# Attention scores of two heads at once on the two row halves of the TensorE array

## The chip, the cores and the metric

The kernel runs on one NeuronCore of one Trainium2 chip. A core has a matrix engine (TensorE, written PE in the profile, with its weight loads shown as PEld), three engines for elementwise work (VectorE or DVE, ScalarE or ACT, GpSimd or POOL), a queue that issues transfers (SyncE or SP), a working memory (SBUF) of 128 partitions, and an accumulation memory (PSUM) of eight banks, each 128 partitions by 512 float32 columns. The metric is the device time of one execution in microseconds, taken as the median of several runs.

## The reference, cut to what matters

The program is one layer of a hybrid decoder: a feed-forward block, then a mixer of two branches (a gated linear attention, GLA, and a stick-breaking attention), then a second feed-forward block, with root-mean-square norms around each. It handles 512 prompt tokens with 16 meta tokens in front of them, and 8 running sequences of 4 new tokens each with 256 cached positions. The change touches the stick-breaking attention of the prompt, which has 16 heads of 64 dimensions:

```python
z = jnp.einsum('bqhd,bkhd->bhqk', qblk, k).astype(jnp.float32) * scale + bias_f
mask = k_idx[None, :] < qi[:, None]
l = jnp.where(mask, jax.nn.log_sigmoid(-z), 0.0)
r = lax.cumsum(l, axis=3, reverse=True) - l
a = jnp.where(mask, jnp.exp(jax.nn.log_sigmoid(z) + r), 0.0)
return jnp.einsum('bhqk,bkhd->bqhd', a.astype(v.dtype), v)
```

So for each head the score of a query and an earlier key is a product over 64 dimensions; its sigmoid is multiplied by the product of (1 - sigmoid) over all keys between the two. All tensors are float32.

## The kernel before

Float32 products are made on TensorE from the type fp32r. A value x is split in two parts: a high part, which is x cast to fp32r, and a low part, which is x minus the high part. A product of x and y is then high by high, high by low and low by high; the fourth is left out. The cast that makes a high part runs on ScalarE (`S.copy`) or VectorE, and the subtraction that makes the low part on VectorE (the helper `tt`, line 172, which is why so many rows of the profile carry L172).

The attention works on pairs of heads: `class Pair` (line 1902), eight pairs. The 128 rows of a pair's query, key and value matrices are two heads of 64 rows, head e = 0 in partitions 0 to 63 and head e = 1 in 64 to 127 (`own_`, line 1885). Projections fill most of TensorE's time in this stage: `tile_steps` (lines 728, 729 and 731 of the profile; queries) takes 8 steps of six matmuls, and `seven_steps` (lines 1079 to 1081; values and keys of one pair together, with seven products of half matrices in place of eight) 14 steps of six matmuls. The work of the pair before, everything between its scores and its weighted values, is placed between these steps.

Order is written out by hand. All of TensorE, VectorE, ScalarE and GpSimd run inside `manual_schedule`: each engine executes in the order in which the program emits its instructions. At each step of the projections the program emits six matmuls, then what `later(n, f)` has due (counted in steps from the call), then the list `at[n]`, whose entries are kept in the order in which they were registered with `then`. The loop at line 2555 registers, for pair `pr`, its own pieces at n + d with n = BEGIN[pr+1], and the weight preparation of the pair's projections at BEGIN[pr] + TILE + d. Two entries for one step stand in the order of the loop: the pieces of pair `pr` first, the weight preparation of pair `pr+1` after them. Of that preparation (`weights_at`, line 1041) three places matter here. The cast of the block called "b2" (128x1024, ScalarE, line 1006) is emitted at n + 10 and its low part (VectorE) at n + 11; the matmuls that read b2 first are those of step n + 15. A block called "t4" (128x512) is cast at n + 13 and its low part made at n + 15. The samples of the queries are copied at n + 11 (line 1926), and a partial sum of the projection, e5, at n + 12 on ScalarE (line 1059).

For the scores, each query block i of 128 tokens meets 144, 272, 400 or 528 keys (16 meta tokens and the tokens up to its own end), 1344 columns in all for a head, laid out in three PSUM banks of 416, 416 and 512 columns (`PARTS`, `BANKS`, lines 1868 to 1871). `scores(e, n)` (line 1996) makes bank n of head e: five segments of a head (144, 272, 400, 16 and 512 columns) with two matmuls each, 20 matmuls a pair. Each uses all 128 rows of the array. The query tile of a head holds its high part in the head's own 64 partitions and its low part in the other 64; the key tile holds the key's high part twice. One matmul therefore sums high by high and low by high. The second takes a tile `klz` with the key's low part in the head's own half and zeros in the other. So one pass of 64-row products is saved by stacking, at the price of copies between halves: `hi` and `lo` of the queries and `key_parts` of the keys each run twice, once a head, on 64 partitions.

Behind the scores come two sigmoids a bank on ScalarE (`keep` and `beta`, lines 2012 and 2013, `keep` with single columns zeroed by GpSimd), a running product along the keys on VectorE (`scan`, line 2026, in two parts of 416 and 928 columns), `weigh` (beta times the shifted product, 1343 columns, L172, then two copies of the meta columns, line 2036), and then ten 128x128 transposes a head (`turned`, line 2087) and the product with the values (`summed`, line 2103, at the third step of the next pair, followed by `meta_summed`, line 2118). `rows_v`, `rows_k` and `tails` (lines 2053, 2042, 2062 to 2064) transpose keys and values into output rows; `tails` is followed by four short VectorE operations (lines 2068 to 2075). The steps are:

```python
pieces = [(3, now.scores, 0, 0), (3, now.scores, 0, 1), (4, now.meta), (5, now.scan, 0, 0),
          (6, now.scores, 0, 2), (6, now.scores, 1, 0), (6, now.rows_v), (8, now.scan, 0, 1), (9, now.scan, 1, 0),
          (10, now.weigh, 0), (11, now.scores, 1, 1), (11, now.scores, 1, 2), (11, now.rows_k), (11, now.tails),
          (14, now.scan, 1, 1), (15, now.weigh, 1)]
```

`turned` follows at step 16 (first head) and 19 (second). For pairs 4 to 7 sixteen transposes of cached keys (`sample_keys`, line 2190) stand at step 14, and for pair 1 a few small matmuls (`sample_rows_out`, lines 2169 and 2171). So TensorE visits the scores three times a pair, at steps 3, 6 and 11. PSUM tiles of the kind `ps` rotate through four banks, and `scores` takes one at a time, two a visit.

Of the kernel before, what the change touches and what calls it, by code (L numbers as in the profile page):

```python
# [9 lines left out]
F32 = mybir.dt.float32  # L10
F32R = mybir.dt.float32r
# [5 lines left out]
P = 128  # L17
# [36 lines left out]
06481820500232254e646b6c0c808e2c42907a388c927e8884706846862a2e1478587644826e5436403e3c246a661e623a948a5b7c100e60545a  # L54
0072741416126a555628262034245a3202305e86462e5c50824458563c403676542a786e07491e3a948a0e62106674607c1812167a726c0c3892
2c708c42078488021d48406a1c238e687e04903c801e065207140900841f16506a231a4a513e681d483d527e19068e810a50214c8014120b183c
1c481e061f2350531968213e8e805117143c0a061281161822526a1e191b80403e1c8f06508e18810a162212401b206a1e3e23068e1a190a8050
1812211b0b6a1e400a0680231a208e181b126a13211420231e06088e0a8030606e7462568c34381a32428a7012667c2a92445a54244e78820f20
0d6c7e8a68483c167052183e0f4e206a500d4012584f0c50703f3d4041513e4f0c503c3d4f7141703c3d3e403f185a2a3e7012504d4a59665806
0a244e480f2894746042863c4456326e14928e6202000482487a5070160c124d7e7c0e1080390b33756187078c72466c0840263d36433f453c57  # L60
29909525676f6a2276784b308a3888544a68344d7e50369052374e843a202212706a4b384a4d367c7d226a4c366c0e804a10168c722e0c2a7c1a
7a1c5e92181e3c8e5c225a602c5707403e6e947466264228468c0a245956877208440c86756a2e1a0620629238406e18024a243e161e47808c1d
669474367210335e0a3a4c3259560e046c26751c7c7a071a946220802e000c385a8645666a8c10061e6044728e2c923c369333320e5c0b088274
5e06601e942220475f2a62581c287a6c7c09241a6a488c102b262c44928e7256576e168136804218747a64146b0b0402084c0e3e40327c866c28
3c8209101a5a8e728c669281566a26242b4236010c181000083b3e824c440e4a484d242826423c402c2e36010c48284618080a2b2411823e4d2e
0244043b42002c183c40080a36480c4200020411483b26824d180a2c2e2b4c39370824283e3c0c422b0037404336243b824a053c0a0818024539
3e11280e0c004c480440422b370c2826242f3e11484a36822d002b0c0e0a083c241802054244262b824c2d10360042251840043b3c2f484a102b
82000208260a24282d0e0c0536102b394c82403642002b0d183c3e3b3802000c39288236080e100a404a4c242639363e2882040c3c2b42364818
263e243c4345264202000c28408210484c0a080e824a26280c4004362b2d0a48943e1e284c42100c2f62185a925d1a2d803a3862944524080a43
3c585f2c4a06805c940e822648422a1e1862432c3e4062485a1a2e80925c45245d18431e4a2a425e5c2c620608621824940a82260e5e5a1a4562  # L70
5c182c48240e4c0c4a1e2810185c2a5e421a4582264428182e2c461e1f2010224846441c4c0c4a605e1e2a2e2c0e1928100c222f20261c188248
4c2a4a4644422e0e2c181c1f00281e8094830a1a063c109204083e373a0082405826281e203b38390236102200920c0e83382c6263245a820302
26629237002c823a05040212243060725e5c5a62644e847e687a8e76887c706e526c78030174666a8c8a9406420a2a864408804b912d8a181a3c
2c54561c3e49020048904636502a2c2d0e8220729222024486803903014b605810707c0c00946a0942028c400b08074b0174526e66008c786d6c
00067a7b8f8889768448730f93117d412e5a7e71610d21644c5c1e624e482a7e6c8a4a043c1a5602543e361878008c50908643121680846a9426
7628246e74442a66325282228e3058209240085a607a700d5d2f2e3b06125c347c3616733a140888116670432c723b190c2a151a060e0f125a2e
425c3618898838467313082c17431c44120e0a1b72193a5a7336881a435d0c5e5c061c2d2c18151214360a1b171a423a730e5c88897215181406
0c1d2d1c1a380b0e42372c8872163606145d895c1a1c0b060c0a37882c0e365d5c1b421072880608820a50928e6e867e6c48146204361a0c946a
248c303c0276204e2a5474582c2e42465a9056141236181e1a54161c0c44757454587490751912911d181c5490741d581c197559185a0c243875
40563e74373c1c5718594336509082945492  # L80
# [56 lines left out]
def hybrid_step(  # L137
# [1747 lines left out]
    own_, other = (slice(0, 64), slice(64, P)), (slice(64, P), slice(0, 64))  # L1885
# [16 lines left out]
    class Pair:  # L1902
# [9 lines left out]
        def queries(self):  # L1912
# [15 lines left out]
            def hi(e):  # L1928
                if e == 0:
                    self.qs = [take(NP, F32R) for _ in range(2)]  # L1930
                S.copy(self.qs[e][own_[e]], qf[own_[e], :NP])

            def lo(e):
                tt(self.qs[e][other[e]], qf[own_[e], :NP], self.qs[e][own_[e]].bitcast(F32), ALU.subtract)
                if e:
                    give(qf)

            for n, f in ((3, samples), (6, lambda: hi(0)), (8, lambda: lo(0)), (9, lambda: hi(1)), (11, lambda: lo(1))):
                later(n, f)

        def keys(self):
# [7 lines left out]
            for e in range(2):  # L1949
                self.key_parts(e)  # L1950
            self.sample_parts()

        def key_parts(self, e):
            kf = self.kf
            if e == 0:
                self.ks = [take(nk, F32R) for _ in range(2)]
                self.kl = klz
# [842 lines left out]
```

## Time and profile before

| what | value |
|---|---|
| median of 3 runs | 1483.24 us (1483.19 to 1483.31) |
| the profiled execution: its time, its span | 1483.86 us, 1482.2 us |
| granted TensorE clock | 0.999 |
| busy: PE, DVE, ACT, POOL | 1473.1, 1094.1, 819.7, 59.9 us |
| attention of the prompt, 585 to 812 us of the span: PE, DVE, ACT busy | 227.0, 189.7, 175.1 us |

Spans and starts are microseconds from the first instruction. A matmul's row gives its start, its length from start to the last result, and its tile's shape as rows*columns of the weights and partitions x columns of what streams through. Matmuls overlap: a 280-column matmul shows 0.29 us, but the next starts about 0.13 us after it. The cost of a piece of work in the stream is therefore read from the end of the matmul before it to the end of the first one behind it.

### The profile page before, as it was taken

To read this page: it belongs to the slowest core of one execution; us is meant where nothing else is said; L and a number is where in the kernel's file an instruction comes from. 1 tells how busy PE (TensorE), PEld (TensorE's weight loads), DVE (VectorE), ACT (ScalarE), POOL (GpSimd) and SP (SyncE) were. 2 spreads that over 40 slices of the span, in tenths; PEclk is the share of its full clock that TensorE was granted. 3 is DMA by queue.
4 is the path that set the end of the run, shared out by engine and by line. 5 is a ranking of instruction groups with operands and counts; after the bars stand their busy time and mean duration, and the time that the engine had idled before them with its cause. 6 is when DMAs were issued, how large, how long until landed. Compare 5 with 4: busy or idle time off the path is not lost.

```text
span 1482.2 us, 29733 instructions
## 1 busy us (share of the span) xinstructions
PE 1473.1 (99%) x11825; PEld 1427.4 (96%) x11825; DVE 1094.1 (74%) x1812; ACT 819.7 (55%) x1537; POOL 59.9 (4%) x177
## 2 busy tenths in 40 slices
PE   9999999999999999999999999999999999999998
PEld 8999999999999889999998999999999999999998
DVE  5888888855677866988887754776577898888544
ACT  7455545534565557777776544644564555455334
POOL 2000000000000111300100000000000000000000
PEclk9999999999999999999999999999999999999999
DMA  8133333324765687567677767334631333333253
GB/s 253 45 100 89 100 99 102 89 79 125 180 134 132 174 146 174 122 119 147 146 136 177 244 136 205 102 91 129 189 105 49 102 96 108 95 108 88 81 148 120
DMA packets 288540, 187.60 MB, mean 127 GB/s; under 512 B 10988, under 2 KB 266674, under 8 KB 288402
## 3 DMA queue, kind: packets, MB, share of 16 engines
q1 hardware_dynamic: 280706, 181.97, 46.1%
q0 software_dynamic: 7680, 3.74, 2.4%
q8 instruction: 93, 1.52, 0.4%
q14 instruction: 45, 0.37, 0.1%
q10 hardware_dynamic: 16, 0.00, 0.0%
HBM read 160.63 MB, written 25.03 MB: 125 GB/s over the span
## 4 chain that ended last, share of the span: by engine, by line
PE 95%; DVE 2%; ACT 2%; DMA 1%; issue 0%; DVEq 0%; SPq 0%; ACTq 0%
PE acc L1302 8%; PE acc L1300 8%; PE acc L1301 8%; PE acc L741 6%; PE acc L742 6%; PE acc L744 6%; PE acc L728 5%; PE acc L729 5%; PE acc L731 5%; PE acc L1079 4%; PE acc L1081 4%; PE acc L1080 4%; PE acc L1242 2%; PE acc L1239 2%; PE acc L1240 2%; PE ps L2103 1%
## 5 line engine op out<-in xcount | busy, mean ns | idle before, releaser
L172 DVE TENSOR_TENSOR room<-room,room 128x544 fp32r<-128x544 f32 (+13 forms) x473 | 303.6, 661 | 87.5 <-ACT room L808 18.7
L172 DVE TENSOR_TENSOR lo<-raw,hi 128x1024 fp32r<-128x1024 f32 (+1 forms) x207 | 248.0, 1199 | 74.1 <-ACT hi L1006 37.1
L1302 PE MATMUL acc<-room,lo 128*128 128x280 f32 (+1 forms) x896 | 259.7, 290 | 0.0
L1300 PE MATMUL acc<-room,hi 128*128 128x280 f32 (+1 forms) x896 | 259.5, 290 | 0.0
L1301 PE MATMUL acc<-room,hi 128*128 128x280 f32 (+1 forms) x896 | 259.2, 289 | 0.0
L1006 ACT CAST hi<-raw 128x1024 fp32r<-128x1024 f32 x114 | 119.5, 1052 | 142.1 <-PE acc L1301 49.2
L728 PE MATMUL acc<-room,hi 128*128 128x280 f32 x608 | 173.2, 302 | 0.2 <-DVE room L175 0.2
L1300 PEld LDWEIGHTS acc<-room,hi 128*128 128x128 f32 x896 | 168.6, 188 | 0.0
L1301 PEld LDWEIGHTS acc<-room,hi 128*128 128x128 f32 x896 | 168.6, 188 | 0.0
L1302 PEld LDWEIGHTS acc<-room,lo 128*128 128x128 f32 x896 | 168.5, 188 | 0.0
L729 PE MATMUL acc<-room,hi 128*128 128x280 f32 x608 | 163.5, 288 | 0.0
L1079 PE MATMUL acc<-room,hi 128*128 128x280 f32 x476 | 141.7, 298 | 1.1 <-ACT acc L1069 0.9
L172 DVE TENSOR_TENSOR lo<-room,hi 128x1024 fp32r<-128x1024 f32 x106 | 101.2, 955 | 52.4 <-ACT hi L1006 52.2
L1081 PE MATMUL acc<-room,lo 128*128 128x280 f32 (+1 forms) x476 | 138.3, 290 | 0.0
L1080 PE MATMUL acc<-room,hi 128*128 128x280 f32 (+1 forms) x476 | 138.1, 290 | 0.0
L706 ACT CAST hi<-raw 128x1024 fp32r<-128x1024 f32 (+1 forms) x93 | 93.6, 1007 | 75.6 <-issue 21.5
L1006 ACT CAST hi<-room 128x1024 fp32r<-128x1024 f32 x106 | 89.1, 840 | 82.1 <-PE acc L1301 61.0
L731 PE MATMUL acc<-room,lo 128*128 128x280 f32 x608 | 125.9, 288 | 0.0
L728 PEld LDWEIGHTS acc<-room,hi 128*128 128x128 f32 x608 | 114.4, 188 | 5.2 <-issue 3.8
L729 PEld LDWEIGHTS acc<-room,hi 128*128 128x128 f32 x608 | 114.6, 189 | 0.3
L741 PE MATMUL acc<-room,hi 128*128 128x280 f32 (+2 forms) x388 | 110.7, 295 | 0.0
L742 PE MATMUL acc<-room,hi 128*128 128x280 f32 (+2 forms) x388 | 108.9, 290 | 0.0
(413 smaller groups left out, 3554.2 us busy)
## 6 DMA issues: line engine op xcount, KB each, us to landing
raw<-in_w_in_dram SPq DMA_DIRECT2D x68, 256.0 KB, 5.5
raw<-in_ffn_w_gate_dram SPq DMA_DIRECT2D x64, 256.0 KB, 3.1
raw<-in_ffn_w_up_dram SPq DMA_DIRECT2D x64, 256.0 KB, 3.3
raw<-in_ffn_w_down_dram SPq DMA_DIRECT2D x36, 448.0 KB, 3.8
raw<-in_w_in_dram SPq DMA_DIRECT2D x29, 512.0 KB, 7.2
out_dram<-room SPq DMA_DIRECT2D x36, 256.0 KB, 4.2
room<-in_cache_k_dram SPq DMA_DIRECT2D x32, 256.0 KB, 7.1
room<-in_cache_v_dram SPq DMA_DIRECT2D x32, 256.0 KB, 5.2
```

Of the source, the lines that this page charges most:

```text
L172: (eng or V).tensor_tensor(out=out, in0=a, in1=b, op=op)
L728: T.matmul(acc[h][:, :w], hi[k], act.get(k, h, w)[0], start=(k == order[0]), stop=False, skip_group_check=True)
L729: T.matmul(acc[h][:, : wid[h]], hi[k], a[h][1], start=False, stop=False, skip_group_check=True)
L731: T.matmul(acc[h][:, : wid[h]], lo[k], a[h][0], start=False, stop=(k == order[-1]), skip_group_check=True)
L741: T.matmul(acc[h][:nw, : wid[h]], wh, a[h][0], start=(k == 0), stop=False)
L742: T.matmul(acc[h][:nw, : wid[h]], wh, a[h][1], start=False, stop=False)
L1006: S.copy(hi[:, :kt], src)
L1079: T.matmul(x[:, :n], hi, act_[k][0][:, :n], start=(first and k == 0), stop=False, skip_group_check=True)
L1081: T.matmul(x[:, :w], lo, act_[k][0][:, :w], start=False, stop=(k == 3), skip_group_check=True)
L1300: T.matmul(x[:, :QW], hi, act[k][0], start=(first and k == 0), stop=False, skip_group_check=True)
L1301: T.matmul(x[:, :QW], hi, act[k][1], start=False, stop=False, skip_group_check=True)
L1302: T.matmul(x[:, :QW], lo, act[k][0], start=False, stop=(k == 3), skip_group_check=True)
```

## The change

The scores use the array as two halves of 64 rows. The tiles of queries and keys keep both heads in their own partitions, one tile for the high parts and one for the low parts. For each segment three products are made (high by high, high by low, low by high), each as two matmuls of 64 rows, head 0 in rows 0 to 63 and head 1 in rows 64 to 127, into two different PSUM banks: 30 matmuls a pair in place of 20. The high and low parts are made with one instruction for both heads, 128 partitions at once, the copies between halves and the zeroed tiles `klz` fall away, and the cast of the keys moves from two on VectorE and two on ScalarE to one on VectorE. A visit to the scores now makes one bank for both heads, at steps 3, 6 and 10; `scan` is in three parts of 416, 400 and 528 columns, `weigh` in two, of 815 and 528 columns. `rows_k` and `tails` move from step 11 to 10. The byte string `PLACES`, which says where in SBUF each tile lies, is replaced as a whole and is left out here.

```diff
-    klz = [take(nk, F32R) for _ in range(2)]
-    for t in klz:
-        G.memset(t.bitcast(F32), 0.0)
...
+    own_ = slice(0, 64), slice(64, P)
+    AT, SCANS = (0, 416, 832), (slice(0, 416), slice(416, 816), slice(816, NW_))
...
-            def hi(e):
-                if e == 0:
-                    self.qs = [take(NP, F32R) for _ in range(2)]
-                S.copy(self.qs[e][own_[e]], qf[own_[e], :NP])
-
-            def lo(e):
-                tt(self.qs[e][other[e]], qf[own_[e], :NP], self.qs[e][own_[e]].bitcast(F32), ALU.subtract)
...
+            def hi():
+                self.qs = [take(NP, F32R) for _ in range(2)]
+                S.copy(self.qs[0], qf[:, :NP])
+
+            def lo():
+                tt(self.qs[1], qf[:, :NP], self.qs[0].bitcast(F32), ALU.subtract)
+                give(qf)
+
+            for n, f in ((3, samples), (6, hi), (9, lo)):
                 later(n, f)
...
-            src, ks = kf[own_[e], NS:], self.ks
-            V.tensor_copy(ks[e][own_[e]], src)
-            S.copy(ks[e][other[e]], src)
-            tt(klz[e][own_[e]], src, ks[e][own_[e]].bitcast(F32), ALU.subtract)
+        def key_parts(self):
+            src = self.kf[:, NS:]
+            hi, lo = self.ks = [take(nk, F32R) for _ in range(2)]
+            V.tensor_copy(hi, src)
+            tt(lo, src, hi.bitcast(F32), ALU.subtract)
...
-            for n, f in ((13, lambda: self.key_parts(0)), (15, lambda: self.key_parts(1)), (16, self.sample_parts)):
+            for n, f in ((14, self.key_parts), (16, self.sample_parts)):
...
-                T.matmul(o, qs[e][:, qc], ks[e][:, kc], start=True, stop=False)
-                T.matmul(o, qs[e][:, qc], kl[e][:, kc], start=False, stop=True)
+                for x, y in ((qh, kh), (qh, kl), (ql, kh)):
+                    for e, r in enumerate(own_):
+                        T.matmul(p[e][:, c : c + k1 - k0], x[r, qc], y[r, kc], start=(x is qh and y is kh), stop=(x is ql))
...
-        def weigh(self, e):
+        def weigh(self, e, n):
             beta, keep = self.wide[e]
-            tt(beta[:, : NW_ - 1], beta[:, : NW_ - 1], keep[:, 1:], ALU.mult)
+            a, b = ((0, 815), (815, NW_ - 1))[n]
+            tt(beta[:, a:b], beta[:, a:b], keep[:, a + 1 : b + 1], ALU.mult)
...
-            pieces = [(3, now.scores, 0, 0), (3, now.scores, 0, 1), (4, now.meta), (5, now.scan, 0, 0),
-                      (6, now.scores, 0, 2), (6, now.scores, 1, 0), (6, now.rows_v), (8, now.scan, 0, 1), (9, now.scan, 1, 0),
-                      (10, now.weigh, 0), (11, now.scores, 1, 1), (11, now.scores, 1, 2), (11, now.rows_k), (11, now.tails),
-                      (14, now.scan, 1, 1), (15, now.weigh, 1)]
+            pieces = [(3, now.scores, 0), (4, now.meta), (5, now.scan, 0, 0), (6, now.scan, 1, 0), (6, now.scores, 1), (6, now.rows_v),
+                      (8, now.scan, 0, 1), (9, now.weigh, 0, 0), (10, now.scan, 1, 1), (11, now.weigh, 1, 0),
+                      (10, now.scores, 2), (10, now.rows_k), (10, now.tails),
+                      (13, now.scan, 0, 2), (14, now.weigh, 0, 1), (15, now.scan, 1, 2), (16, now.weigh, 1, 1)]
```

More of the change, by code (lines that the diff above doesn't have):

```diff
@@ L78 @@
[L78 to L80 removed]
+365a540c320824203012147a62827c44426e6672026092886a708e6884947618801c7404864c2a5052904e1f2e066c8a48404a183e3c7e8c2a18
+10156446007828291a2e2a0c201e2c26322428682294840886041c744e527690181a8a803c4a487e386c368c3a5e5c5a643e55167846627c0002
@@ L2586, in hybrid_step @@
         then(n + 21, lambda: give(*qz[:2]))
-        then(n + 23, lambda: give(*vfm, *klz, once.pop("begun"), *(once.pop(t) for t in ("az", "am", "vm"))))
+        then(n + 23, lambda: give(*vfm, once.pop("begun"), *(once.pop(t) for t in ("az", "am", "vm"))))
         for n in range(1 - 2 * MIX0, 1):
```

108 lines of the change are left out of this document (49 added, 59 removed).

## The prediction

> **What bounds the kernel now.** I read the page first, then the busy times of the stretch in which the changed code runs, then the timelines of its engines. The page's busy times, and the windows (PE, PEld, DVE, ACT, POOL busy us, then clock, DMA share, GB/s):
>
> ```profile
> PE 1473.1 (99%) x11825; PEld 1427.4 (96%) x11825; DVE 1094.1 (74%) x1812; ACT 819.7 (55%) x1537; POOL 59.9 (4%) x177
> 585.00:812.00 227.00, 227.00 (x1849) 210.27 (x1849) 189.69 (x309) 175.10 (x338) 28.35 (x89) 1.00 0.67 141
> ```
>
> TensorE is busy for all of the 227 us, so time is won or lost in two ways only: by what its own stream costs, and by a wait put into it. ScalarE and VectorE lose three instructions a pair each (a query part and, of the keys, two copies here, a cast and a low part there), and VectorE gets four shorter ones more (two scans, two products). I cost both at nothing, since TensorE's stream covers them. Since the stage moves at PE's pace, order matters here more than load.
>
> **The three visits as they are**, pair 3 (timeline of PE: start, length):
>
> ```profile
> 665.41 0.41 PE L731 MATMUL acc<-room,lo 128*128 128x280 f32 x2
> 665.75 2.37 PE L2103 MATMUL ps<-room,room 128*64 128x512 f32 x16
> 668.06 0.50 PE L2118 MATMUL ps<-room,room 96*128 96x512 f32 x1
> ...
> 669.37 0.38 PE L728 MATMUL acc<-room,hi 128*128 128x280 f32 x1
> ...
> 671.46 0.41 PE L731 MATMUL acc<-room,lo 128*128 128x280 f32 x2
> 671.71 0.40 PE L2008 MATMUL ps<-room 128*128 128x512 f32 x1
> 671.95 0.40 PE L2009 MATMUL ps<-room,room 128*128 128x512 f32 x1
> 672.18 0.23 PE L2008 MATMUL ps<-room,room 128*128 128x144 f32 x1
> 672.66 0.60 PE L2053 MATMUL ps<-ident,room 128*128 128x128 f32 x4
> ...
> 676.78 0.29 PE L1081 MATMUL acc<-room,lo 128*128 128x280 f32 x1
> 676.91 0.34 PE L2008 MATMUL ps<-room,room 128*128 128x400 f32 x1
> 677.10 0.35 PE L2009 MATMUL ps<-room,room 128*128 128x400 f32 x1
> 677.28 0.17 PE L2008 MATMUL ps<-room,room 128*128 128x16 f32 x1
> 677.31 0.26 PE L2009 MATMUL ps<-room,room 128*128 128x16 f32 x1
> 677.42 0.48 PE L2008 MATMUL ps<-room,room 128*128 128x512 f32 x1
> 677.97 0.60 PE L2042 MATMUL ps<-ident,room 128*128 128x128 f32 x4
> ```
>
> From end to end: first 668.56 to 669.75, less 0.13 for the 280-column matmul behind it, 1.06 us; second 671.87 to 673.26, less 0.44 for four transposes of 0.11, 0.95; third 677.07 to 678.57, less 0.44, 1.06. Together 3.07 us a pair. The steps are 0.23 for 512 columns (671.71, 671.95, 672.18), 0.18 for 400 (676.91, 677.10, 677.28), 0.13 for 280 (676.78 to 676.91), which I take for 272 too, and never under 0.11 behind a short matmul (677.31 to 677.42), where the next weights are what is waited for; 144 columns get 0.11.
>
> **What a visit will cost.** The trace has no pair of 64-row halves. Its nearest rows are two 64-column halves side by side (L2103), and a matmul on a part of the rows (16 of them, L456); L804 and L805 give the price of plain float32:
>
> ```profile
> 611.54 0.64 PE L2103 MATMUL ps<-room 128*64 128x512 f32 x1
> 611.55 0.64 PE L2103 MATMUL ps<-room,room 128*64 128x512 f32 x1
> ...
> 385.20 0.29 PE L744 MATMUL acc<-room,lo 128*128 128x280 f32 x1
> 385.33 0.63 PE L804 MATMUL ps<-room,ones 128*128 128x280 f32 x2
> 385.80 0.64 PE L805 MATMUL ps<-room,ones 128*128 128x280 f32 x2
> 386.06 0.50 PE L741 MATMUL acc<-room,hi 128*128 128x280 f32 x1
> ...
> 484.08 0.41 PE L731 MATMUL acc<-room,lo 128*128 128x280 f32 x2
> 484.42 0.69 PE L456 MATMUL ps<-room 16*128 16x256 f32 x2
> 485.05 0.40 PE L728 MATMUL acc<-room,hi 128*128 128x280 f32 x1
> ```
>
> L804 and L805: 385.49 to 386.56, less 0.13, is 0.94 us for 4 x 280 columns, 0.84 ns a column. The column halves start 0.01 us apart, and the sixteen of a pair of heads (512, 384, 256 and 128 columns, twice each a head) take 665.82 to 668.56, less 0.23 for L2118, 2.51 us. One head's 2560 columns at 0.84 ns are 2.15, so the second head costs nothing; 0.36 is over. I take the same for row halves (bounds: one price for two heads, as here, and both heads in turn). L456: 484.49 to 485.45, less 0.13, is 0.83 us for 2 x 256 columns, which at 0.84 ns are 0.43. The other 0.40 us is what it costs to leave the whole array and come back: the stream runs dry and weights are loaded in the open, twice. No such cost shows between shapes of the whole array above. Bounds: nothing, and 0.40 a visit; I take 0.40, as L456 is the row with part of the rows.
>
> The Trainium skill, TensorEngine Tiling (Array Packing), section Key Properties, says that changing the tiling mode drains TensorE; the 0.40 us agrees, and it names no mode that is exempt.
>
> Sum of a pair, three products for each segment: first visit 3 x 0.11 + 3 x 0.13 = 0.72, second 3 x 0.18 + 2 x 0.11 + 0.01 = 0.77, third 3 x 0.23 = 0.69, and 3 x 0.40: 3.38 us against 3.07. So the visits lose 0.31 us a pair, **2.5 us** in eight. The three saved passes of 1344 columns are real; three drains a pair eat them.
>
> **What the new order costs.** The scores of the third bank now stand at step 10, in front of the cast of b2 on ScalarE, which is registered for step 10 by the next turn of the loop; before, the sigmoids came at 11, behind it. ScalarE, VectorE, PE, same pair:
>
> ```profile
> 672.38 0.69 ACT L2012 ACTIVATE room<-ps,sbb 128x512 f32<-128x512 f32 x1 [0.21 <-PE ps L2009]
> 676.68 1.06 ACT L1006 CAST hi<-raw 128x1024 fp32r<-128x1024 f32 x1
> 678.62 0.70 ACT L2012 ACTIVATE room<-ps,sbb 128x512 f32<-128x512 f32 x1
> 679.19 0.71 ACT L2013 ACTIVATE room<-ps,sbb 128x512 f32<-128x512 f32 x1
> 679.76 0.61 ACT L2044 COPY room<-ps 128x512 f32<-128x512 f32 x1
> ...
> 679.97 1.23 DVE L172 TENSOR_TENSOR lo<-raw,hi 128x1024 fp32r<-128x1024 f32 x1
> ...
> 681.32 0.33 PE L1081 MATMUL acc<-room,lo 128*128 128x280 f32 x1
> ```
>
> The b2 low part ends at 681.20 and its first reader (step 15, third matmul) starts at 681.32: 0.12 us to spare already. Let E be the moment at which the matmul behind the third visit starts (677.97 here). PE reached that reader 3.35 us after E, with three steps between; with one step more (six matmuls of 0.13) it is E + 4.13. ScalarE starts on the bank 0.20 after E (672.18, 672.38); four sigmoids of 0.57 (678.62, 679.19, 679.76), the copy of `rows_k` 0.47 (0.61 less the 0.14 by which such neighbours overlap), the cast 1.06, and VectorE's low part 1.23 give E + 5.24. PE waits **1.1 us**. Behind that cast on ScalarE stands the copy of e5, which the first matmul of step 15 waits for with 280 columns; VectorE's low part of 1.23 us, which runs beside it, takes longer, so it lies inside the same wait. VectorE then has the scan of 528 columns and the product of 528, which end in front of the fourth transpose of `turned` at step 16:
>
> ```profile
> L2026 DVE TENSOR_TENSOR_SCAN room<-room,room 128x928 f32<-128x928 f32 x16 | 33.3, 2084 | 0.0
> L2026 DVE TENSOR_TENSOR_SCAN room<-room,room 128x416 f32<-128x416 f32 x16 | 16.2, 1012 | 10.9 <-POOL room L2016 10.8
> L172 DVE TENSOR_TENSOR room<-raw,raw 128x512 f32<-128x512 f32 x9 | 6.2, 686 | 0.5 <-PE ps L2103 0.5
> 707.53 1.91 PE L2190 MATMUL ps<-ident,room 128*128 128x128 f32 x16
> 627.02 1.03 PE L2171 MATMUL ps<-ones,room 1*128 1x1 f32 x8
> ```
>
> The scan is 1.25 (1.01 plus 112 columns at 2.1 ns), the product 0.70, less 0.1 of overlap: E + 7.1, while PE, off again at 5.24, is there after four matmuls, a step and three transposes (0.52 + 0.78 + 0.33) at 6.9. Another 0.2; **1.3 us a pair** in all. Pairs 4 to 7 have L2190's 1.9 us at step 14, ahead of the reader: no wait there. Pair 1 has L2171 and its transpose, 1.1 us: 0.3 is left. So pairs 0, 2 and 3 pay 1.3 and pair 1 0.3, **4.2 us**. Bounds: nothing, and 1.3 in all seven pairs that have a b2 behind them, 9.1.
>
> The rest I cost at nothing. The six instructions that fall away on ScalarE and VectorE would give, without PE's cover, at most 6 x 0.69 us a pair (the 512-column row). Both heads' first scores now need all of the keys at step 3 and the cast comes one step later for head 0, but `summed` (2.4 us) stands ahead of them on PE. PSUM still gives two banks a visit, in the same turn. The new byte string of places moves no instruction.
>
> Sum: 2.5 + 4.2 = 6.7 us. The profiled execution had a span of 1482.2 us and a time of 1483.86, 1.7 around the span and 0.6 above the median of 1483.24; I expect 1488.9 of span, about 1490.6 for its time, and a median of **1490.0 us**.
>
> **Rivals.**
> R1, no wait at step 15: the order is as read, but ScalarE and VectorE have run further ahead than I give them. For it: PE waits nowhere in this stretch now. Against: the chain starts at scores that PE itself makes. 1483.2 + 2.5 = 1485.7.
> R2, the other side, changing to row halves is free. Place: both ends of each visit. Price: 24 x 0.40 = 9.6 us less, 1480.4, and some exposed loads back, 1481. It decides from 0.12 us a visit down, where 24 x 0.12 pays for what is left of the waits (6.7 - 9.6 + 24s = 0). For it: L456 is a matmul alone, without a partner. Against: L2103's 0.36, with partners.
> R3, the halves' weight loads are not hidden. Streams alone are 0.56 us for five segments (1344 columns at 0.42 ns), three times 1.68, plus 15 loads of 0.11, 1.65, plus 1.2: 4.53, 1.15 more a pair, 9.2 in eight: 1499.2. The row
>
> ```profile
> 677.10 0.19 PEld L2008 LDWEIGHTS ps<-room,room 128*128 128x128 f32 x1
> ```
>
> speaks against it: on the whole array a load starts while L2008's matmul of 676.91 (0.34 long) runs. The Trainium skill, TensorE: Matmul & The Clock Gate, section The mechanism, has loads overlap with running matmuls only where the row group differs; that is R3 for a half's second load; for the whole array the trace disagrees, and no run here shows it for halves.
> R4, the change doesn't do what it says: the heads run in turn. Then streams and steps double, 2 x 2.18 + 1.2 = 5.56, 2.18 more a pair: 1507.
> R5, R1 and R2 together: 1481 - 4.2 = 1477.
>
> **How the numbers follow.** Forecast 0.42, R1 0.16, R2 0.13, R3 0.12, R4 0.07, R5 0.06, 0.04 for what I don't see. A measurement here tells 0.2%, 3.0 us, from no change. Faster (below 1480.3): R5, a third of R2, some of the rest, 0.14. The same (to 1486.2): most of R1 and of R2, 0.21. Slower: 0.65. The range of 8 in 10 takes in R1, R2 and R3, 1481 to 1500; the forecast's own, with waits of 2 to 9 us, is 1487 to 1495.
>
> **What would show it.** Rows of 64*128 matmuls with both heads' starts 0.01 to 0.02 us apart (R4: a step of 0.11 or more); a visit of 1.1 to 1.2 us end to end with a dry PEld at both ends (R2: 0.7); PE waiting for VectorE's low part at L1081 once a pair in pairs 0, 2 and 3, near 1 us, and not in 4 to 7 (R1: none). I am wrong if the visits come out shorter than 1 us, or if PE waits at another place.

## The result and the profile after

The changed kernel takes 1492.2 us (median of 4 runs, 1492.2 to 1493.64) against 1483.23 us before (4 runs, 1483.19 to 1483.31): the ratio is 1.0063, 95% interval 1.0045 to 1.0080. It is slower, as forecast, by 2.2 us more than forecast (1490.0). The span of the profiled execution went from 1482.2 to 1490.5 us, 8.3 more; its time, 1492.2, is the median itself, while the profiled execution of before lay 0.6 above its median.

From the page of the changed kernel its busy line, and from the windows the same stretch as before (us, then PE, PEld, DVE, ACT, POOL busy, clock, DMA share, GB/s):

```profile
PE 1477.0 (99%) x11905; PEld 1421.8 (95%) x11905; DVE 1085.3 (73%) x1820; ACT 804.9 (54%) x1513; POOL 57.0 (4%) x175
585.00:812.00 227.00, 223.13 (x1807) 198.43 (x1806) 176.81 (x310) 156.24 (x302) 24.09 (x83) 1.00 0.65 132
```

The work that was to go is gone: VectorE is busy 8.8 us less, ScalarE 14.8 us less. None of it shows in the time: TensorE, which was busy for all of the 227 us, now stands idle for 3.9 of them. The view of TensorE's waits from 580 to 820 us (before: none) says for whom (total us, times, longest):

```profile
PE ps L2078 <- ACT room L2183: 1.7, 1, 1.7
PE acc L1081 <- DVE lo L172: 1.3, 3, 0.4
PE acc L1079 <- ACT room L1059: 0.7, 3, 0.3
```

The second was forecast, three times, in pairs 0, 2 and 3; the third stands in the same pairs, where the prediction had it inside the second. The first, once, in pair 7, was not forecast.

**Where the 8.3 us are.** The first matmul of `summed` (512 columns on column halves) ends the work of one pair and begins that of the next, so its start is a milestone. Timelines of TensorE, first the kernel before, then the changed one, each with the first score matmul of pair 0 on top:

```profile
587.71 0.23 PE L2008 MATMUL ps<-room 128*128 128x144 f32 x1
...
721.61 0.64 PE L2103 MATMUL ps<-room 128*64 128x512 f32 x1
...
780.35 0.65 PE L2103 MATMUL ps<-room,room 128*64 128x512 f32 x2
...
807.33 0.65 PE L2103 MATMUL ps<-room,room 128*64 128x512 f32 x2
```

```profile
587.39 0.45 PE L1996 MATMUL ps<-room 64*128 64x144 f32 x4
...
612.76 0.65 PE L2094 MATMUL ps<-room,room 128*64 128x512 f32 x2
...
726.84 0.64 PE L2094 MATMUL ps<-room,room 128*64 128x512 f32 x1
...
786.16 0.65 PE L2094 MATMUL ps<-room,room 128*64 128x512 f32 x2
...
815.55 0.65 PE L2094 MATMUL ps<-room,room 128*64 128x512 f32 x2
```

Pairs 5 and 6 took 58.74 us (721.61 to 780.35) and now take 59.32: 0.29 more each, with no wait in them. Pair 7 took 26.98 and takes 29.39, 2.41 more; pair 0 took 23.83 (587.71 to the 611.54 of the prediction) and takes 25.37, 1.54 more. Worked out in the same way from one profiled execution of each kernel, for all eight pairs and the runs below (each is told in the next section), the growth of each pair over the kernel before, in us:

| kernel | 0 | 1 | 2 | 3 | 4 | 5 | 6 | 7 | sum |
|---|---|---|---|---|---|---|---|---|---|
| changed kernel | 1.54 | 0.38 | 1.72 | 1.64 | 0.27 | 0.29 | 0.29 | 2.41 | 8.5 |
| e2 cast first | 1.37 | 0.17 | 1.48 | 1.45 | 0.27 | 0.30 | 0.28 | 4.00 | 9.3 |
| e3 cast, product first | 0.21 | 0.18 | 0.30 | 0.34 | 0.27 | 0.29 | 0.29 | 3.94 | 5.8 |
| e4 extra visit | 1.91 | 0.70 | 2.06 | 1.95 | 0.61 | 0.66 | 0.61 | 2.73 | 11.2 |
| e8 other place | 1.54 | 0.38 | 1.71 | 1.62 | 0.26 | 0.30 | 0.29 | 1.16 | 7.3 |
| e5 two visits | 1.68 | 1.24 | 1.91 | 1.90 | 0.29 | 0.24 | 0.28 | 5.53 | 13.1 |
| e6 heads in turn | 2.31 | 1.14 | 2.46 | 2.40 | 1.02 | 1.03 | 1.03 | 3.16 | 14.6 |
| e7 whole array | 1.16 | -0.11 | 1.17 | 1.12 | 0.04 | 0.03 | 0.03 | 1.86 | 5.3 |
| e9 all | 3.80 | 2.71 | 4.12 | 3.96 | 0.83 | 1.01 | 0.51 | 2.94 | 19.9 |
| e10 waits out | 0.22 | 0.17 | 0.30 | 0.34 | 0.27 | 0.30 | 0.28 | 1.99 | 3.9 |
| e12 keep place | 0.22 | 0.17 | 0.33 | 0.34 | 0.26 | 0.30 | 0.28 | 0.63 | 2.5 |
| e13 keep place, products early | 0.03 | -0.13 | 0.30 | 0.27 | -0.09 | -0.03 | -0.05 | 0.63 | 0.9 |

The sum begins at the first score matmul, which the profiles have between 587.3 and 588.7 us; what lies ahead of it is left out of the table. The two latest starts are e5 (588.67) and e9 (588.32); why is not shown. e11, left out of the table, lies between e10 and e13 with a sum of 1.5.

**Both heads at once.** The third visit of pair 3, TensorE and its weight loads:

```profile
679.79 0.73 PE L1996 MATMUL ps<-room 64*128 64x512 f32 x4
680.36 0.39 PE L1996 MATMUL ps<-room,room 64*128 64x512 f32 x2
680.68 0.55 PE L2033 MATMUL ps<-ident,room 128*128 128x128 f32 x3
```

```profile
679.79 0.30 PEld L1996 LDWEIGHTS ps<-room 64*128 64x128 f32 x4 [0.15 <-issue]
680.13 0.19 PEld L1996 LDWEIGHTS ps<-room,room 64*128 64x128 f32 x2
680.67 0.42 PEld L2033 LDWEIGHTS ps<-ident,room 128*128 128x128 f32 x4 [0.36 <-ACT acc L1069]
```

The last two of six products of 512 columns start 0.57 us after the first; one by one, at the prediction's step of 0.23, it would be 1.15. Four weight loads are done in 0.30 us, while the first matmuls run. So the heads run side by side and the loads within the visit are hidden: R4 and R3 fall, on the spot. At both ends of the visit the loads stand dry, as the prediction said they would: 0.15 us before its first load and 0.36 before the first one behind it.

**Pair 3, the forecast wait.** ScalarE, VectorE and TensorE:

```profile
683.08 0.61 ACT L2035 COPY room<-ps 128x512 f32<-128x512 f32 x1
683.54 1.09 ACT L1006 CAST hi<-raw 128x1024 fp32r<-128x1024 f32 x1
684.50 0.42 ACT L1059 COPY room<-acc 128x280 f32<-128x280 f32 x1
```

```profile
683.24 1.01 DVE L172 TENSOR_TENSOR room<-room,room 128x815 f32<-128x815 f32 x1
684.28 0.37 DVE L2025 COPY room<-room 128x96 f32<-128x96 f32 x1
684.66 1.23 DVE L172 TENSOR_TENSOR lo<-raw,hi 128x1024 fp32r<-128x1024 f32 x1
```

```profile
684.44 0.29 PE L1081 MATMUL acc<-room,lo 128*128 128x280 f32 x1
684.97 0.40 PE L1079 MATMUL acc<-room,hi 128*128 128x280 f32 x1 [0.24 <-ACT room L1059]
685.21 0.29 PE L1080 MATMUL acc<-room,hi 128*128 128x280 f32 x1
685.94 0.40 PE L1081 MATMUL acc<-room,lo 128*128 128x280 f32 x1 [0.44 <-DVE lo L172]
686.18 0.29 PE L1079 MATMUL acc<-room,hi 128*128 128x280 f32 x1
```

The low part of b2 ends at 685.89, 5.21 us behind E (680.68); the prediction had 5.24. But two chains reach it at the same moment: the cast on ScalarE ends at 684.63, and VectorE comes from head 1's first product and its small copy at 684.65.

The idle times in brackets, 0.24 and 0.44 us, are less than what the wait costs. In an unbroken stream these matmuls start 0.13 us apart; here the four steps are 0.53, 0.24, 0.73 and 0.24, together 1.2 us more. That is why 3.9 us of idle time and the longer visits make up 8.5 us of growth.

**Pair 7, the wait that was not forecast.** VectorE, ScalarE, TensorE:

```profile
802.97 1.25 DVE L2015 TENSOR_TENSOR_SCAN room<-room,room 128x528 f32<-128x528 f32 x1
804.14 1.20 DVE L172 TENSOR_TENSOR lo<-raw,hi 128x1024 fp32r<-128x1024 f32 x1
805.25 0.70 DVE L172 TENSOR_TENSOR room<-room,room 128x528 f32<-128x528 f32 x1
```

```profile
806.07 2.05 ACT L2183 COPY room<-ps 128x512 f32<-128x512 f32 x4 [3.77 <-DVE room L172]
```

```profile
806.71 1.52 PE L2078 MATMUL ps<-ident,room 128*128 128x128 f32 x10 [1.72 <-ACT room L2183]
```

ScalarE's copy of the transposed sample keys stands idle for 3.77 us until VectorE has done the last product of head 0 (805.25 + 0.70). The new list of places puts this copy where head 0's `keep` lies, and `weigh` gives `keep` back only behind that product, which the new order has at step 14 (the kernel before made the whole product at step 10). Behind the copy stand the banks of PSUM that the transposes of `turned` need.

### The profile page after: what moved, and what is told of

Its sections match the earlier page's. It is cut to its first block, busy times and chain, and to the rows that moved or that the text cites. A ratio compares the mean times of both kernels' runs of the same rounds, so it can differ in the third digit from the quotient of the medians.

```text
span 1490.5 us, 29845 instructions
## 1 busy us (share of the span) xinstructions
PE 1477.0 (99%) x11905; PEld 1421.8 (95%) x11905; DVE 1085.3 (73%) x1820; ACT 804.9 (54%) x1513; POOL 57.0 (4%) x175
## 4 chain that ended last, share of the span: by engine, by line
PE 94%; DVE 3%; ACT 1%; DMA 1%; issue 0%; SPq 0%; DVEq 0%; ACTq 0%
PE acc L1300 8%; PE acc L1301 8%; PE acc L1302 8%; PE acc L741 6%; PE acc L744 6%; PE acc L742 6%; PE acc L728 5%; PE acc L729 5%; PE acc L731 5%; PE acc L1079 4%; PE acc L1081 4%; PE acc L1080 4%; PE acc L1242 2%; PE acc L1239 2%; PE acc L1240 2%; PE ps L1996 1%
## 5 line engine op out<-in xcount | busy, mean ns | idle before, releaser
L172 DVE TENSOR_TENSOR room<-room,room 128x560 fp32r<-128x560 f32 (+12 forms) x470 | 294.0, 645 | 84.2 <-ACT room L1059 17.0
L1079 PE MATMUL acc<-room,hi 128*128 128x280 f32 x476 | 141.9, 298 | 2.1 <-ACT room L1059 1.1
```

Of the source, the lines that this page charges most:

```text
L172: (eng or V).tensor_tensor(out=out, in0=a, in1=b, op=op)
L1079: T.matmul(x[:, :n], hi, act_[k][0][:, :n], start=(first and k == 0), stop=False, skip_group_check=True)
```

## The experiments

Times are medians of five rounds beside the kernel before on the same chip (1483.25 to 1483.48 us there). The expectations were written before each run.

**e2, the cast of b2 early.**

```diff
-t=(-3, -2), b2=(2, 3), t4=(5, 7)
+t=(-3, -2), b2=(1, 3), t4=(5, 7)
```

> The cast of b2 on ScalarE is registered one step earlier and so stands in front of the third visit's sigmoids again; all else is as in the changed kernel. My theory: the low part of b2 is late by two chains at once, ScalarE's (four sigmoids, the copy of rows_k, the cast of 1.1 us) and VectorE's (the tails, which wait for the transposes behind the scores, the samples, the product of head 1, then the low part of 1.23 us). With the cast early, VectorE's own order still makes the low part end about 4.9 us after the third visit: the wait of about 1.45 us in pairs 0, 2 and 3 falls to about 1.0, the one for the copy of e5 goes. About 1.3 us less than the changed kernel, 1490.9 us. Rival, ScalarE's order alone makes the wait: all 4.6 us go, 1487.6 us. Rival, the waits are no cost of the order at all: no change, 1492.2 us.

Measured: 1491.44 us, ratio 1.0051 (1.0038 to 1.0065). Pair 3 of this kernel, ScalarE's cast, VectorE, TensorE:

```profile
678.87 1.09 ACT L1006 CAST hi<-raw 128x1024 fp32r<-128x1024 f32 x1
```

```profile
682.78 1.01 DVE L172 TENSOR_TENSOR room<-room,room 128x815 f32<-128x815 f32 x1
...
683.95 1.22 DVE L172 TENSOR_TENSOR lo<-raw,hi 128x1024 fp32r<-128x1024 f32 x1
```

```profile
685.22 0.40 PE L1081 MATMUL acc<-room,lo 128*128 128x280 f32 x1 [0.68 <-DVE lo L172]
```

The cast is done 4 us before the low part begins, the wait for e5's copy is gone, and TensorE still waits, now 0.68 us at one place: pairs 0 to 3 are shorter by 0.17 to 0.24 us each, 0.8 in all (expected 1.3). ScalarE's order alone is not the cause. That pair 7 is longer here is told in the last section.

**e3, the cast and head 1's first product early.** Beside e2's edit:

```diff
-(10, now.scan, 1, 1), (11, now.weigh, 1, 0),
+(10, now.scan, 1, 1), (10, now.weigh, 1, 0),
```

> As the run with the cast of b2 early, and the first product of head 1 (beta times keep, 815 columns, 1.0 us on VectorE) moved from step 11 to step 10, ahead of the third visit's scores, so that it no longer stands between the tails and the low part of b2. My theory: both chains are short again, the waits at the low part, at the copy of e5 and at the fourth transpose of turned go in pairs 0 to 3: 4.6 us less than the changed kernel, 1487.6 us, and the waits in pair 7 stay. Rival, TensorE waits for something else next (VectorE's tails or the scan of 528 columns): 1489 to 1492 us.

Measured: 1488.32 us, ratio 1.0031 (1.0019 to 1.0043), 3.9 us below the changed kernel. Pairs 0 to 3 come down to 0.21, 0.18, 0.30 and 0.34, the level of pairs 4 to 6: the two edits together take out 4.25 us (expected 4.6). Of TensorE's waits from 580 to 830 us one is left, in pair 7, the same 1.7 us for ScalarE's copy as in the changed kernel. Head 1's product early without the cast early was not run.

**e4, one visit more.** The first visit's two segments at steps 3 and 4:

```diff
-pieces = [(3, now.scores, 0), (4, now.meta)
+pieces = [(3, now.scores, 0, 0), (4, now.scores, 0, 1), (4, now.meta)
```

> The first visit of a pair (segments of 144 and 272 columns) is cut in two: the first segment's six products at step 3, the second segment's six and the sigmoids at step 4, with the products of another chain between them. The same products and loads; only one more change from the whole array to the halves and back, eight times in all. My theory, a change and the way back cost about 0.38 us: 8 x 0.38, 3.0 us more than the changed kernel, 1495.2 us. Rival, the change is free and what a visit costs is loads and columns: no change, 1492.2 us, or 0.1 us a visit, 1493.0 us.

Measured: 1495.54 us (expected 1495.2), ratio 1.0079 (1.0066 to 1.0093). Milestones at the ends of pairs 4 and 6:

```profile
728.68 0.64 PE L2102 MATMUL ps<-room,room 128*64 128x512 f32 x1
...
788.69 0.65 PE L2102 MATMUL ps<-room,room 128*64 128x512 f32 x2
```

60.01 us for two pairs against 59.32: 0.35 us a pair for a change from the whole array to the halves and back; in the table the eight pairs have 0.31 to 0.36. R2, that it is free, falls.

**e5, two visits.** The second visit, products and sigmoids, at step 3:

```diff
-pieces = [(3, now.scores, 0), (4, now.meta)
+pieces = [(3, now.scores, 0), (3, now.scores, 1), (4, now.meta)
-(6, now.scan, 1, 0), (6, now.scores, 1), (6, now.rows_v)
+(6, now.scan, 1, 0), (6, now.rows_v)
```

> The second visit's products and sigmoids move from step 6 to step 3, right behind the first visit's, so that a pair of heads has two visits to the row halves and not three; the products are the same. My theory: one change to the halves and back a pair is saved, 8 x 0.38, 3.0 us less than the changed kernel, 1489.2 us, if the two banks more that are open at once make TensorE wait nowhere. Rival, the change is free: no change, 1492.2 us. Rival, four sigmoids more at step 3 hold up ScalarE's casts: a wait of 0.5 us or more a pair takes the gain back, 1493 us or more.

Measured: 1497.98 us, ratio 1.0096 (1.0080 to 1.0111): 5.8 us slower than the changed kernel where 3.0 faster was expected. ScalarE and TensorE in pair 3:

```profile
675.29 0.61 ACT L2001 ACTIVATE room<-ps,sbb 128x416 f32<-128x416 f32 x1 [0.32 <-PE ps L1996]
...
679.22 1.10 ACT L1006 CAST hi<-room 128x1024 fp32r<-128x1024 f32 x1
```

```profile
688.67 0.40 PE L1081 MATMUL acc<-room,lo 128*128 128x280 f32 x1 [1.03 <-DVE lo L172]
```

Eight sigmoids in a row keep ScalarE 3.9 us from the next cast; VectorE's scans slide back and so does b2's low part. The third rival, named with 1493 us or more, is what came; e9 and e11 take the two effects apart.

**e6, the heads in turn.**

```diff
+for e, r in enumerate(own_):
+    c = 0
     for i, k0, k1 in BANKS[n]:
         for x, y in ((qh, kh), (qh, kl), (ql, kh)):
-            for e, r in enumerate(own_):
-                T.matmul(...)
+            T.matmul(...)
```

> The products of a visit are issued head by head (all of head 0's on the upper rows, then all of head 1's on the lower rows) in place of one of each in turn; number, shape and visits are the same. My theory: in the changed kernel the two heads' products run at once, so in turn their columns and steps count twice. The steps of a pair, 2.2 us, are paid once more: 8 x 2.2, some 17 us more, 1509 us; if TensorE still lets the first products of head 1 start beside the last of head 0 where they meet, 2 to 4 us less than that. Rival, the halves did not run at once in the changed kernel either: no change, 1492.2 us.

Measured: 1498.45 us, ratio 1.0102 (1.0087 to 1.0118): 6.2 us over the changed kernel, not 17. Parts of the second and then of the third visit of pair 3 (a row under one shape can hold 16-column products too):

```profile
677.96 0.63 PE L1997 MATMUL ps<-room 64*128 64x400 f32 x2
678.43 0.34 PE L1997 MATMUL ps<-room,room 64*128 64x400 f32 x1
678.44 0.63 PE L1997 MATMUL ps<-room 64*128 64x400 f32 x4
...
683.06 0.73 PE L1997 MATMUL ps<-room 64*128 64x512 f32 x4
683.64 0.40 PE L1997 MATMUL ps<-room,room 64*128 64x512 f32 x2
```

The third visit has three products of head 0 and then three of head 1, and takes about as long as in alternation: 683.06 to 684.04, 0.98 us, against 0.96 (679.79 to 680.75). In the second, six of head 0 stand first, and head 1's first starts at 678.44, with head 0's third. Both agree with TensorE taking a matmul on idle rows up to three places ahead of its turn. A visit then costs more only by what head 0 does before head 1 begins: 0.48 us in the second (677.96 to 678.44), 0.30 in the first (674.30 to 674.60), 0.01 in the third. Each of pairs 4 to 6 is 0.74 us longer than in the changed kernel, times eight 5.9.

**e7, the new order on the whole array.**

```diff
-for x, y in ((qh, kh), (qh, kl), (ql, kh)):
-    for e, r in enumerate(own_):
-        T.matmul(p[e][...], x[r, qc], y[r, kc], ...)
+for e in range(2):
+    for y in (kh, kl):
+        T.matmul(p[e][...], qh[:, qc], y[:, kc], ...)
```

> The new order of the steps with products on the whole array: for each segment and head two products of 128 rows (queries times keys, queries times low part), 20 a pair as in the kernel before, in place of 30 on the halves. The scores that it computes are the sums over both heads, and the third product is left out, so the output is not the reference's. My theory: no change of the array's mode, so the visits cost what they cost before, 3.06 us a pair in place of 3.28: 8 x 0.23, 1.8 us less than the changed kernel, 1490.4 us, and still 6.5 to 7 us above the kernel before, from the waits in pairs 0 to 3 and 7. Rival, the visits on the halves cause the waits or make up most of the loss: 1483 to 1486 us.

Measured: 1488.96 us (expected 1490.4), ratio 1.0037 (1.0024 to 1.0051). Milestones at the ends of pairs 4 and 6:

```profile
724.82 0.64 PE L2094 MATMUL ps<-room,room 128*64 128x512 f32 x1
...
783.62 0.65 PE L2094 MATMUL ps<-room,room 128*64 128x512 f32 x2
```

58.80 us, 0.03 a pair over the kernel before. So the visits on the halves cost 0.26 us a pair (2.1 in eight). 5.3 us of the sum of 8.5 are left here and come with the new order and places. The other 1.2 us, which the expectation did not have, are waits that are shorter here: in the views of TensorE's waits, 2.1 us in pairs 0, 2 and 3 fall to 1.5 and the 1.7 in pair 7 to 1.4. So the visits on the halves lengthen the waits as well; how was not followed.

**e8, other places for the last pair's keys.**

```diff
 list of places, entries 878 to 881
-76 74 70 56
+56 80 70 76
```

> Four bytes of the list of places are changed: of the four buffers that the transposed keys of the last pair are copied into, the first no longer lies where the keep of head 0 was, which VectorE's last product of that head gives back only at step 14, and the second lies there no longer either; the third and the fourth do. No instruction is added, removed or moved. My theory: the 2.1 us that TensorE stands still in the last pair come from ScalarE's copy, which waits 3.8 us for the place; with the late places used third and fourth the wait falls to about 0.9 us: 1.2 us less than the changed kernel, 1491.0 us. Rival, the list of places costs nothing and the copy is late for its order on ScalarE: no change, 1492.2 us.

Measured: 1491.68 us, ratio 1.0054 (1.0040 to 1.0067). Pair 7 is 1.25 us shorter in the profile (1.16 for 2.41), as expected; the median shows 0.5 (scatter 1491.17 to 1492.41), too little to tell by itself. No instruction is touched, so the places make that part of the wait.

**e9, three edits.** e3's, e5's and e8's.

> Three edits together: the cast of b2 and head 1's first product earlier, the other places for the last pair's keys, and the second visit's products at step 3 with the first's. My theory: 4.6 us of waits in pairs 0 to 3, 1.2 us of the wait in pair 7 and eight changes of mode at 0.38 go: 1492.2 - 4.6 - 1.2 - 3.0 = 1483.4 us, the same as the kernel before (1483.2). Rival, the gains overlap or new waits appear at step 3: 1485 to 1490 us.

Measured: 1502.89 us, ratio 1.0127 (1.0112 to 1.0143), the worst of all (expected 1483.4). The expectation added e5's gain before e5 was known. Pairs 0, 2 and 3 wait over 2 us each and pair 1 waits 1.0, and behind each of these waits the clock is halved for 3.41 us (rows in the last section).

**e10 and e11, all waits out, and the products alone early.** e10 is e3, e8's places, and in pair 7 the last scan and product of head 0 one step earlier. e11 adds the second visit's products at step 3, its sigmoids left at 6:

```diff
-(13, now.scan, 0, 2), (14, now.weigh, 0, 1)
+(13 - (pr == 7), now.scan, 0, 2), (14 - (pr == 7), now.weigh, 0, 1)
-pieces = [(3, now.scores, 0), (4, now.meta)
+pieces = [(3, now.products, 0), (3, now.products, 1), (3, now.scores, 0), (4, now.meta)
```

> The three edits that take waits away, together: the cast of b2 one step earlier and head 1's first product ahead of the third visit (they took 3.9 us by themselves), the other places for the last pair's keys (0.5 us by itself), and in the last pair the last scan and product of head 0 one step earlier (12 and 13 for 13 and 14), so that the place is given back before ScalarE's copy needs it. The visits are those of the changed kernel. My theory: the change is made of 1.8 us of visits, 4.6 us of waits in pairs 0 to 3 and 2.1 us in the last pair; only the visits are left: 1483.3 + 1.8 to 2.4, 1485.1 to 1485.7 us, and no wait of TensorE over 0.3 us from the first scores to the end of the last pair. Rival, the waits move elsewhere: 1487 us or more.

> As the run with all waits out, and the second visit's products (not its sigmoids) moved from step 6 to step 3, right behind the first visit's; the sigmoids stay where they are, four at step 3 and four at step 6, and two banks of PSUM stay taken for three steps. My theory: where both moved, the merged visit was 0.32 us shorter than the two, and what made that kernel slower was eight sigmoids in a row, not the products. So 8 x 0.32, 2.6 us less than the run with all waits out: 1482.5 to 1483.2 us, the same as the kernel before. Rival, the two banks held make TensorE wait for PSUM between steps 3 and 6: 0.5 us a pair or more, 1487 us or more.

Measured: e10 1487.15 us, ratio 1.0025 (1.0015 to 1.0034); e11 1485.15, ratio 1.0013 (1.0004 to 1.0022). e11 is 2.0 us faster than e10 (expected 2.6); the time that it was given, 1482.5 to 1483.2 us, was missed along with e10's. Against e9, which differs in pairs 0 to 6 by the place of the second visit's sigmoids alone, it has none of the long waits: it was e5's sigmoids that cost, not its products. e10 missed its 1485.1 to 1485.7, its rival of 1487 us or more came, and its profile has 1.3 us of waiting left in pair 7, for this row of ScalarE:

```profile
801.77 1.56 ACT L2183 COPY room<-ps 128x512 f32<-128x512 f32 x3 [3.32 <-DMA out_dram<-room]
```

The place that e8 had chosen for the second copy was under a transfer to DRAM.

**e12 and e13, a better place.** e10 and e11 with the second copy where `keep` was:

```diff
-56 80 70 76
+56 76 70 74
```

> As the run with all waits out, with other bytes for the four places of the last pair's transposed keys: the second copy goes to a place of head 0's keep, which there is given back at 800.3 us, and no longer to a place whose last reader is a transfer to DRAM that ends only at 801.7. My theory: the 1.3 us that TensorE still waited for ScalarE's copy in the last pair go: 1487.15 - 1.3, 1485.8 us. Rival, the copy is late for another reason than its place: no change, 1487.2 us.

> The same places in the run with the second visit's products at step 3. There TensorE waited 0.7 us for that copy: 1485.15 - 0.7, 1484.4 us. If the theory of the loss is whole (1.8 us of visits, less 2.6 us for the saved change of mode, no waits), it should be at 1482.5 to 1484.5 us; the kernel before is at 1483.25. Rival, something else of the change costs 1 us or more: 1485 us or more.

Measured: e12 1486.29 us (expected 1485.8), ratio 1.0020 (1.0011 to 1.0029); e13 1484.88 (expected 1484.4, at most 1484.5), ratio 1.0008 (0.9999 to 1.0017). In e12 the copy starts earlier, behind VectorE, and the view of TensorE's waits from 580 to 830 us is empty. ScalarE:

```profile
801.19 1.57 ACT L2183 COPY room<-ps 128x512 f32<-128x512 f32 x3 [1.97 <-DVE room L172]
```

With these waits out the change still loses 2.5 us by the table (3.0 by the medians), 0.27 a pair in pairs 0 to 6. In e13, with one visit fewer, its milestones

```profile
722.14 0.64 PE L2101 MATMUL ps<-room,room 128*64 128x512 f32 x1
...
780.80 0.65 PE L2101 MATMUL ps<-room,room 128*64 128x512 f32 x2
```

are 58.66 us apart for two pairs, 0.04 a pair under the kernel before. In pairs 2 and 3 the saved visit gains only 0.03 and 0.07 us: there the fourth transpose of `turned` starts later behind the third (in pair 3 0.36 us, in e12 0.24). Its time can hardly be told from the kernel before (1.6 us over it, an interval that just reaches 1). The table explains 0.9 of the 1.6; the profile of before, on which the table rests, lies 0.6 above its own median, and the rest stays open. No version was faster than the kernel before.

## Why the prediction was right or wrong

**Visits, forecast 2.5 us: the mechanism right, a size a little high.** The three products of a segment run at the price of one head, loads hidden, and what eats the saved passes is the change from the whole array to halves and back. It was priced at 0.40 us from L456; e4 shows 0.35, e13 against e12 0.33 (58.66 for 59.32 us, halved). By the prediction's own way of reading, the three visits of pair 3 take 1.11, 1.13 and 1.04 us, 3.28 together for its 3.38; none is under the 1 us that it named as a sign of being wrong. The growth of a pair is 0.27 on the mean of pairs 0 to 6 of e12 (forecast 0.31), 2.2 us in eight. R2 would have needed 0.12 us or less.

**Waits behind the new order, forecast 4.2 us: right in sum, short in its chain, and so in part by luck.** The growth of pairs 0 to 3 over e12's is 1.32, 0.21, 1.39 and 1.30 us, 4.2 together, where 1.3, 0.3, 1.3 and 1.3 stood; pairs 4 to 6 have none, as said. The step that was incomplete is the chain of four sigmoids, the copy of `rows_k`, the cast and VectorE's low part: it gave VectorE nothing to do until the cast ends. VectorE has the tails, the samples and head 1's first product to do, and comes free 0.02 us after the cast (684.65 and 684.63). ScalarE's chain had its right length; that VectorE's was no longer was luck. One number came out of two chains: e2 shows that shortening ScalarE's is not enough, e3 that shortening both is. That VectorE's alone would not do follows from the rows (the cast ends at 684.63 all the same), and no run shows it. Also the wait is split: 0.24 of the 0.68 us of idle time stand at L1079, for the copy of e5, which the prediction put inside the other.

**Places, forecast nothing: wrong, 2.1 us.** "The new byte string of places moves no instruction" is true and does not follow through: a place that is given back late holds the instruction that takes it. Pair 7 grew by 2.41 us where the other pairs without waits grew by 0.27. It is shown by e8 (1.25 us less for four bytes) and by e12 against e10, which differ by places alone (pair 7 from 1.99 to 0.63). Of the 0.36 us that e12 still has over 0.27, all stands between the transposes of `turned` (two steps of 0.25 and 0.21 us where 0.11 is usual, each with a longer step behind it), and no run shows its cause. Late giving back comes from the new order, so place and order make this wait together; the order by itself was not run. The prediction named this as a sign of being wrong: "or if PE waits at another place".

**Why the time was under-forecast by 2.2 us.** The span grew by 8.3 us where 6.7 were forecast, 1.6 more: 2.1 for the places, less 0.3 for the visits and 0.2 at both ends of the stretch. The other 0.6 is no work of the kernel: the forecast put the median 0.6 us under the profiled execution, as in the kernel before, and here the two are the same.

**The work saved on ScalarE and VectorE, costed at nothing:** right; 23.6 us less of it, and the time rises by what TensorE's stream and waits gained.

**Rivals.** R1 (no wait) holds for pairs 4 to 6, not for the time. R3 and R4 fall by the rows of the visits, R4 also by e6, R2 and R5 by e4.

The sum that the runs give is 2.2 (visits) + 4.2 (pairs 0 to 3) + 2.1 (pair 7), 8.5 us, the growth in the table. The span shows 8.3, since the scores began 0.32 us earlier in the profile of the changed kernel (587.39 for 587.71) and 0.1 came behind the last milestone.

## What to carry to other kernels

Splitting the array pays by the columns it saves and cost 0.33 to 0.35 us here for each visit between matmuls on the whole array (one visit more in e4, one fewer in e13): put the products of several visits into one, but leave the work that follows them on other engines spread out (e11 against e9). When steps move, follow every engine's own queue to the same instruction, since two chains can end together and mending one then gives little (0.8 us in e2, 4.25 in e3). A new plan of buffers is part of the order of execution: ask of each late-freed buffer who takes it next.

## What was not expected of the hardware

**TensorE takes up a matmul on idle rows ahead of its turn.** e6 shows it by up to three places. The Trainium skill, TensorE: Matmul & The Clock Gate, section Step-by-step: what each phase is for, has only weight loads pulled ahead and matmuls in program order; the rows of e6 disagree for matmuls on different row halves.

**A stall can halve the clock afterwards.** In e3 TensorE stood for 1.72 us in pair 7 (800.98 to 802.70), and a little later the clock was halved for 3.41 us; the same came four times in e9, of which two are shown (the windows run from the beginning to the end of each dip, and the third number from their end is the clock):

```profile
803.71:807.12 3.41, 3.41 (x23) 1.81 (x23) 1.22 (x4) 2.25 (x6) 0.00 (x0) 0.50 1.01 195
```

```profile
603.36:606.77 3.41, 3.35 (x15) 3.34 (x15) 3.27 (x6) 0.00 (x0) 0.00 (x0) 0.50 1.12 121
634.08:637.49 3.41, 3.41 (x17) 3.40 (x17) 3.24 (x8) 0.27 (x1) 0.00 (x0) 0.50 1.17 174
```

Half the clock for that long is 1.7 us lost. Pair 7 of e2 and e3 has grown by 4.0 and 3.9 us with it, against 2.4 in the changed kernel, whose stall is as long (1.72) and whose clock stayed at 1.00.

The traces part the two by where the stall lies on a fixed beat. The four dips of e9 begin at 603.36, 634.08, 664.80 and 695.52 us, 30.72 apart, nine times 3.4133. Each trace also has the clock halved at its very end, and the dips of e2, e3 and e5 begin 200 times 3.4133 us before that (e3: 803.71 and 1486.38). Counted back from its end in the same way, the trace of the changed kernel has a beat at 806.21 (its end is halved from 1488.87 on), which cuts its stall (804.99 to 806.71) into 1.22 and 0.50 us; the stalls of e4 and e6, 1.71 and 1.70 us and without a dip, are cut too (1.10 and 1.35 us at most in one stretch of 3.41). Those of e2 and e3 lie whole between two beats. In this stage a dip began at the next beat wherever TensorE had stood for 1.72 us or more between two beats (e2, e3, e5 and three times in e9), and not where it had stood for 1.40 (e7) or less. One case breaks this, a stall of 1.01 us in e9 with a dip behind it; between the same two beats stand eight matmuls that stream a single column (631.34 to 632.37), which may count as standing. What is counted is not shown.

That the changed kernel's one run of 1493.64 us, 1.44 over the others, is such a dip fits in size but was not shown. The Trainium skill, same page, section What's actually happening, has the clock halved after a window of 3.4 us without work, counted freely; the length of the dip and the fixed beat agree, while here about half a window of standing was enough.
